# A two-layer decoder trunk on one core: memory gates computed in the order of use, value products on two PSUM tags, first query transpose one token block later

## The chip, the cores and the metric

The kernel runs on one core of a Trainium2 chip. The metric is the device time of one launch in microseconds, as the median of repeated runs. The core's engines are TensorE (PE in the profile; PEld is its weight load), VectorE (DVE), ScalarE (ACT), GpSimd (POOL) and SyncE (SP, which here only starts transfers).

## What is computed

One sequence of 1024 tokens with 1024 features goes through two layers. Both have memory cross-attention: 4 heads of width 128 in which every token reads 256 memory tokens, with a gate per token and feature behind it.

```python
def even_layer(h, mem, ...):          # layer 0
    u = rms_norm(h, norm_g)
    aq, ak, av, az, bh, bc, bb, bz, xq, xz = split(u @ w_in)
    ya = differential_attention(aq, ak, av, ...)    # 8 heads
    yb = short_gated_conv(bh, bc, bb, ...)
    yx = memory_cross_attention(xq, mem, ...)       # 4 heads
    y = concatenate([ya * silu(az), yb * silu(bz), yx * silu(xz)])
    return h + y @ w_out

def odd_layer(h, mem, ...):           # layer 1
    u = rms_norm(h, norm_g)
    cq, ck, cv, cz, cf, xq, xz = split(u @ w_in)
    yc = forgetting_attention(cq, ck, cv, cf, ...)  # 12 heads, q and k normalised
    yx = memory_cross_attention(xq, mem, ...)
    y = concatenate([yc * silu(cz), yx * silu(xz)])
    return h + y @ w_out

def memory_cross_attention(q, mem, mem_g, w_mem_kv, q_g, k_g):
    mk, mv = split(rms_norm(mem, mem_g) @ w_mem_kv)
    q, mk = rms_norm(q), rms_norm(mk)               # per head
    p = softmax(einsum('bshd,bmhd->bhsm', q, mk) * X_DIM ** -0.5)
    return einsum('bhsm,bmhd->bshd', p, mv)
```

## The kernel before

**Numbers and tiles.** Every fp32 operand of a product is split into a rounded high part and the rest (a cast by ACT, a subtraction by DVE or POOL, L130 and L131), and every product is three matmuls: high by high, high by low, low by high. L224 to L226 are the triple of a projection with tokens on the output's partitions (`token_unit`: 8 token blocks of 128, 8 triples each), L257 to L259 that of a projection with features on them (`feature_unit`: two halves of 512 tokens, 8 triples each, used for the gates), L417 the scores, L464 to L466 the value products, L786 to L788 the output projection.

**PSUM.** The 8 banks are dealt to four tags: d has three (projections and output projection), s two (scores), t two (transposes), o one (value products). Tiles of one tag take its banks in the order in which the program names them: a tile gets a bank when the tile that had it has been read, and no later tile of the tag overtakes it.

```python
PSUM_BUFS = {"d": 3, "s": 2, "t": 2, "o": 1}
o = self.bank("po", "o")                                   # pv, L441
```

**A memory pair** (`x_pair`, two pairs of two heads in each layer) projects the queries of both heads (8 token blocks, 128x256), computes both heads' gates (`gate_unit` to `gate_half`: a tanh `th` by ACT, L280, and a product into `xgate` by DVE, L281; the half with tokens 512 to 1023 first, that with tokens 0 to 511 second), and then attends in four groups g of 256 tokens, both heads in turn (`x_attend`). A group of a head is: two score triples, two row maxima (`nm`, DVE L654), two exponentials (`ex`, ACT L656), two reciprocals and scalings (DVE L658, L659), four transposes into one bank (`pt`, PE L451), its split (`pth` by ACT, `ptl` by DVE), six value matmuls into `po`, and `gated_y` (DVE L477), which multiplies `po` by `xgate` into `y`; a transfer from SP takes `y` to DRAM. The groups 0 and 1 need the gate's half of tokens 0 to 511.

**The order.** A scheduler with a timeline simulation of its own fixes each engine's order when the kernel is built: attention is preferred to projections (PRIO_ATT), evacuations of projections to both (PRIO_EVAC). On the chip each engine runs its list in that order and waits where an operand isn't there. While a pair's attention runs, the scheduler fills PE with the next projection: in pair 0 that of pair 1, in pair 1 the output projection.

**The end of layer 0.** While pair 1 runs, transfers bring the output weights in pieces (`wraw`), and ACT casts them into tiles that include the ones from which `u`, the layer's normalised input, was read for the last time (`u<-wraw`, L130). The output projection (`out_proj`) reads `y` back (`yr`), splits it (`yh`, `yl`), and its 24-matmul groups follow.

**The first head of layer 1.** `qkv_unit` projects q, k, v (and the forget logits: 396 columns for head 0) block by block. `evac` and `qk_norm` take a block out of PSUM and normalise it (ACT, DVE L294 and L297, POOL); behind each second block `later(DEFER, ...)` puts the transposes of both blocks (`qk_transpose`, PE L306, from `qr`) two groups of matmuls later. Here layer 0's last token block is still being turned (PE L148) while head 0 is projected: `turn_last`, behind the matmuls of block 2.

Of the kernel before, what the change touches and what calls it, by code (L numbers as in the profile page):

```python
# [7 lines left out]
F32 = mybir.dt.float32  # L8
# [7 lines left out]
P = 128  # L16
T = 1024
# [7 lines left out]
DEFER = 2  # L25
# [8 lines left out]
class Trunk:  # L34
# [178 lines left out]
    def token_unit(self, weights, lhs_hi, lhs_lo, nblk, post, together=False):  # L213

        nc = self.nc
        wh, wl = weights
        n = wh[0].shape[1]
        step = nblk if together else 1
        for t0 in range(0, nblk, step):
            blks = [(tb, self.bank("pd", "ds"[tb % 2] if together or self.boot else "d"), lhs_hi(tb), lhs_lo(tb)) for tb in range(t0, t0 + step)]  # L220
            for k in range(KC):
                h, l = wh[k], wl[k]
                for tb, ps, ah, al in blks:
                    nc.tensor.matmul(ps[:, :n], lhsT=ah(k), rhs=h, start=(k == 0), stop=False)  # L224
                    nc.tensor.matmul(ps[:, :n], lhsT=ah(k), rhs=l, start=False, stop=False)  # L225
                    mm = nc.tensor.matmul(ps[:, :n], lhsT=al(k), rhs=h, start=False, stop=(k == KC - 1))  # L226
            for tb, ps, _, _ in blks:
                with self.tc.high_priority(PRIO_EVAC):
                    post(tb, ps)
            if self.turn_last is not None and t0 == 2:  # L230
                with self.tc.issue_after(mm.ins):
                    self.turn_last()
                self.turn_last = None
            self.tick()

    def u_lhs(self, part):
        def f(tb):
# [23 lines left out]
                post(half, ps)  # L261
            self.tick()

    def gate_unit(self, w, c0, own=None):

        nc = self.nc
        if own is None:
            gate = {half: self.pk.tile([P, 512], F32, name="gate", tag="gate", bufs=2) for half in (1, 0)}
        else:
            gate = {half: own[:, half * 512:(half + 1) * 512] for half in (1, 0)}  # L270

        def post(half, ps):
            self.gate_half(gate[half], ps)
        self.feature_unit(w, c0, post, halves=(1, 0))
        return [gate[half][:, o:o + 256] for half in (0, 1) for o in (0, 256)]

    def gate_half(self, out, ps):
# [157 lines left out]
                                               op0=ALU.add, op1=ALU.max, accum_out=acc)  # L435
                prev[m] = acc

    def pv(self, g, es, vh, vl, nkb, causal):

        nc = self.nc  # L440
        o = self.bank("po", "o")  # L441
        for j in range(nkb // 2):
            pt = self.bank("pt", "t")
            last = causal and 2 * j + 2 == nkb
# [7 lines left out]
            w = 384 if last else 512  # L452
# [27 lines left out]
    def qkv_unit(self, w, cols, ng, gs, g, extra=None, pairs=False, weights=None):  # L480
        nc = self.nc
        qh, ql, kh, kl, vh, vl = self.att_tiles("qh", "ql", "kh", "kl", "vh", "vl")
# [3 lines left out]
        def post(tb, ps):  # L486
# [6 lines left out]
            if tb % 2:  # L493
                if pairs:
                    self.later(DEFER, lambda: self.qk_transpose_pairs(qns[tb - 1:tb + 1], (qh, ql), (kh, kd, kl, kz), g, (tb - 1) * P))
                else:
                    self.later(DEFER, lambda: self.qk_transpose(qns[tb - 1:tb + 1], [(qh, ql, g), (kh, kl, None)], (tb - 1) * P))
        if weights is None:
# [115 lines left out]
    def x_pair(self, layer, pr, w, cq, cz, w_out):  # L614
# [17 lines left out]
        for s, q in enumerate(((q0h, q0l), (q1h, q1l))):  # L632
            head = 2 * pr + s
            xh, xl = mem[s]
            vh, vl = [(lambda kb, v=v: v[:, M + kb * P:M + (kb + 1) * P]) for v in (xh, xl)]
            gate = self.gate_unit(w, cz + head * P, self.p1.tile([P, T], F32, name="xgate", tag="E2", bufs=2))
            heads.append((head, self.terms3(q, ([xh], [xl])), vh, vl, gate))
        if pr == 1:
            self.out_early(w_out)
# [6 lines left out]
    def x_attend(self, layer, g, head, terms, vh, vl, gate):  # L646
# [3 lines left out]
        for qb in (2 * g, 2 * g + 1):  # L650
# [7 lines left out]
            nc.vector.reciprocal(out=rl[:, 0:1], in_=ls[:, 0:1])  # L658
            nc.vector.tensor_scalar(out=e, in0=e, scalar1=rl[:, 0:1], scalar2=None, op0=ALU.mult)  # L659
            es.append(e)  # L660
        o = self.pv(g, es, vh, vl, 2, False)
        self.gated_y(layer, 12 + head, g, o, gate)


# [260 lines left out]
```

## Time and profile before

| | us |
|---|---|
| median of 3 runs (2204.52 to 2206.93) | 2206.74 |
| the profiled execution | 2204.26 |
| its span in the trace | 2202.2 |
| PE busy | 2167.8 (98%) |
| DVE, ACT, POOL busy | 1240.5, 1053.2, 1020.3 |

The mean granted clock of TensorE over the span is 0.996 of full speed. The page's chain of work that ended last runs through PE for 91% and through transfers for 4%. So PE sets the time, and what is left to look at are the stretches in which it waits: by stretches of 50 us, PE is busy for 50.00 of 50 nearly everywhere between 150 and 2150 us, and the exceptions are few. The kernel's places on that axis: the memory pairs of layer 0 from about 840 to 950, its output projection to about 1090, the first head of layer 1 from 1100, and the memory pairs of layer 1 from about 1945.

### The profile page before, as it was taken

The numbers are of one execution on the slowest core, as the hardware profiler recorded it, in microseconds if no ns is written. First come the engines' busy times: TensorE is split into PE (matmuls) and PEld (weight loads), VectorE is DVE, ScalarE is ACT, GpSimd is POOL, SyncE is SP. The second block draws the span as 40 slices with busy tenths as digits, with TensorE's granted clock in tenths as the row PEclk, the third lists the DMA queues.
The fourth block names the chain that finished last, engine by engine and source line by source line (L and its number), as shares of the span: only waits on it lengthen the run. The fifth ranks groups of instructions, "written<-read, shape, count | busy, mean of one in ns | idle before, by whom it ended". The sixth has DMA issues, their size and how long they took to land.

```text
span 2202.2 us, 35113 instructions
## 1 busy us (share of the span) xinstructions
PE 2167.8 (98%) x12528; PEld 1968.7 (89%) x12528; DVE 1240.5 (56%) x2864; ACT 1053.2 (48%) x2503; POOL 1020.3 (46%) x1352
## 2 busy tenths in 40 slices
PE   8999999999999999999999999999999999999999
PEld 7889889899898899778889999999999999998887
DVE  5656756665674677654445554554545555566532
ACT  6656455464554555433334444444444444455321
POOL 5565555555555454342334555544555554522100
PEclk9999999999999999999999999999999999999999
DMA  5450210211202112387521222201122220223743
GB/s 163 138 156 19 62 52 19 73 34 47 61 29 58 37 54 88 116 270 216 187 63 35 58 58 59 63 23 53 48 56 68 58 62 25 65 73 113 232 132 102
DMA packets 216983, 182.99 MB, mean 83 GB/s; under 512 B 19516, under 2 KB 174300, under 8 KB 216808
## 3 DMA queue, kind: packets, MB, share of 16 engines
q1 hardware_dynamic: 193768, 138.80, 21.6%
q10 hardware_dynamic: 23040, 41.95, 6.2%
q8 instruction: 98, 1.61, 0.3%
q14 instruction: 77, 0.63, 0.1%
HBM read 153.32 MB, written 27.38 MB: 82 GB/s over the span
## 4 chain that ended last, share of the span: by engine, by line
PE 91%; DMA 4%; DVE 1%; POOL 1%; ACT 1%; issue 1%; SPq 0%; ACTq 0%; POOLq 0%; DVEq 0%
PE pd L225 11%; PE pd L224 11%; PE pd L226 11%; PE pss L417 8%; PE pd L258 7%; PE pd L257 7%; PE pd L259 7%; PE pd L788 5%; PE pd L786 5%; PE pd L787 5%; PE pt L451 4%; PE po L466 2%; PE po L465 2%; PE po L464 2%; PE pt L306 1%; DMA wraw<-in_e_w_out_dram 1%
## 5 line engine op out<-in xcount | busy, mean ns | idle before, releaser
L224 PE MATMUL pd<-wqh,u 128*128 128x384 f32 (+2 forms) x1504 | 502.2, 335 | 0.7 <-ACT u L130 0.7
L225 PE MATMUL pd<-wql,u 128*128 128x384 f32 (+2 forms) x1504 | 500.8, 333 | 0.1
L226 PE MATMUL pd<-wqh,u 128*128 128x384 f32 (+2 forms) x1504 | 500.8, 333 | 0.0
L225 PEld LDWEIGHTS pd<-wql,u 128*128 128x128 f32 x1504 | 284.2, 189 | 5.8 <-DVE wql L131 0.6
L224 PEld LDWEIGHTS pd<-wqh,u 128*128 128x128 f32 x1504 | 284.1, 189 | 4.8 <-ACT u L130 1.1
L226 PEld LDWEIGHTS pd<-wqh,u 128*128 128x128 f32 x1504 | 283.7, 189 | 4.7 <-DVE u L131 0.2
L257 PE MATMUL pd<-u,wfh 128*128 128x512 f32 x704 | 279.0, 397 | 0.0
L258 PE MATMUL pd<-u,wfl 128*128 128x512 f32 x704 | 278.7, 396 | 0.0
L259 PE MATMUL pd<-u,wfh 128*128 128x512 f32 x704 | 277.8, 395 | 0.0
L131 POOL TENSOR_TENSOR wql<-raw,wqh 128x384 fp32r<-128x384 f32 (+2 forms) x214 | 210.2, 998 | 78.2 <-ACT wqh L130 73.5
L285 ACT ACTIVATE qr<-pd 128x384 f32<-128x384 f32 (+2 forms) x200 | 92.9, 468 | 199.4 <-PE pd L226 198.4
L131 DVE TENSOR_TENSOR yl<-yr,yh 128x512 fp32r<-128x512 f32 x128 | 103.7, 810 | 142.3 <-ACT yh L130 134.2
L124 POOL TENSOR_TENSOR rs_r<-rs_v,neghalf 128x2 f32<-128x2 f32 (+2 forms) x220 | 176.4, 802 | 12.8
L130 ACT ACTIVATE yh<-yr 128x512 fp32r<-128x512 f32 x128 | 80.5, 630 | 207.8 <-PE pd L787 113.4
L130 ACT ACTIVATE pth<-pt 128x512 fp32r<-128x512 f32 (+1 forms) x232 | 121.8, 554 | 112.5 <-PE pt L451 107.4
L131 POOL TENSOR_TENSOR vl<-qr,vh 128x128 fp32r<-128x128 f32 x160 | 79.0, 499 | 206.4 <-ACT vh L130 205.5
L723 POOL TENSOR_TENSOR fbias<-ck,cqn 128x896 f32<-128x896 f32 (+3 forms) x96 | 112.4, 1171 | 131.8 <-DVE mx L434 109.1
L297 DVE TENSOR_TENSOR qr<-qr,rs_r 128x256 f32<-128x256 f32 x200 | 123.5, 618 | 79.8 <-POOL rs_r L124 78.6
L131 POOL TENSOR_TENSOR wfl<-rawf,wfh 128x512 fp32r<-128x512 f32 x88 | 119.6, 1362 | 102.7 <-ACT wfh L130 100.2
L130 ACT ACTIVATE wqh<-raw 128x384 fp32r<-128x384 f32 (+2 forms) x252 | 114.7, 483 | 109.5 <-DMA raw<-in_e_w_in_dram 61.2
L131 DVE TENSOR_TENSOR ptl<-pt,pth 128x512 fp32r<-128x512 f32 (+1 forms) x232 | 143.8, 639 | 34.6 <-ACT pth L130 32.2
L259 PEld LDWEIGHTS pd<-u,wfh 128*128 128x128 f32 x704 | 132.7, 188 | 27.1 <-issue 1.1
(286 smaller groups left out, 5077.5 us busy)
## 6 DMA issues: line engine op xcount, KB each, us to landing
yr<-y_dr ACTq DMA_DIRECT2D x128, 256.0 KB
raw<-in_o_w_in_dram SPq DMA_DIRECT2D x96, 192.0 KB
rawf<-in_e_w_in_dram SPq DMA_DIRECT2D x56, 256.0 KB
y_dr<-y SPq DMA_DIRECT2D x112, 128.0 KB
raw<-in_e_w_in_dram SPq DMA_DIRECT2D x64, 192.0 KB
wraw<-in_e_w_out_dram SPq DMA_DIRECT2D x32, 256.0 KB
rn<-on_dr ACTq DMA_DIRECT2D x32, 256.0 KB
rawf<-in_o_w_in_dram SPq DMA_DIRECT2D x32, 256.0 KB
```

The source lines that it names most:

```text
L124: nc.gpsimd.tensor_tensor(out=r[:, :n], in0=v[:, :n], in1=self.neghalf[:, :n], op=ALU.pow)
L130: nc.scalar.activation(out=hi, in_=src, func=AF.Copy)
L131: lo_eng.tensor_tensor(out=lo, in0=src, in1=f32(hi), op=ALU.subtract)
L224: nc.tensor.matmul(ps[:, :n], lhsT=ah(k), rhs=h, start=(k == 0), stop=False)
L225: nc.tensor.matmul(ps[:, :n], lhsT=ah(k), rhs=l, start=False, stop=False)
L226: mm = nc.tensor.matmul(ps[:, :n], lhsT=al(k), rhs=h, start=False, stop=(k == KC - 1))
L257: nc.tensor.matmul(ps, lhsT=h, rhs=uh[:, k, :], start=(k == 0), stop=False)
L258: nc.tensor.matmul(ps, lhsT=l, rhs=uh[:, k, :], start=False, stop=False)
L259: nc.tensor.matmul(ps, lhsT=h, rhs=ul[:, k, :], start=False, stop=(k == KC - 1))
L297: nc.vector.tensor_tensor(out=v, in0=v, in1=r.unsqueeze(2).broadcast_to([P, ng, gs]), op=ALU.mult)
L417: nc.tensor.matmul(ps, lhsT=q[qb // 4][rows, qs], rhs=k[c0 // 512][rows, ks], start=(i == 0), stop=(i == n - 1))
L723: nc.gpsimd.tensor_tensor(out=b[:, :kext], in0=ck[:, :kext], in1=self.cqn[:, qb, h:h + 1].broadcast_to([P, kext]), op=ALU.subtract)
```

## The change

Three edits. (a) In `x_pair` the gates of the memory heads are computed with the half of tokens 0 to 511 first. (b) The value products of the odd head of each pair take a bank of tag d; those of the even head stay on o. (c) In the first head of layer 1, the transposes of token blocks 0 and 1 come one group later, and are issued behind that group's last matmul. What is computed stays the same, and so does the count of instructions on every engine.

```diff
--- before.py
+++ after.py
@@ -227,11 +227,17 @@
             for tb, ps, _, _ in blks:
                 with self.tc.high_priority(PRIO_EVAC):
                     post(tb, ps)
+            self.group_mm = mm
             if self.turn_last is not None and t0 == 2:
                 with self.tc.issue_after(mm.ins):
                     self.turn_last()
                 self.turn_last = None
             self.tick()
+
+    def behind_group(self, fn, *args):
+
+        with self.tc.issue_after(self.group_mm.ins):
+            fn(*args)
 
     def u_lhs(self, part):
         def f(tb):
@@ -261,7 +267,7 @@
                 post(half, ps)
             self.tick()
 
-    def gate_unit(self, w, c0, own=None):
+    def gate_unit(self, w, c0, own=None, halves=(1, 0)):
 
         nc = self.nc
         if own is None:
@@ -271,7 +277,7 @@
 
         def post(half, ps):
             self.gate_half(gate[half], ps)
-        self.feature_unit(w, c0, post, halves=(1, 0))
+        self.feature_unit(w, c0, post, halves=halves)
         return [gate[half][:, o:o + 256] for half in (0, 1) for o in (0, 256)]
 
     def gate_half(self, out, ps):
@@ -435,10 +441,10 @@
                                                op0=ALU.add, op1=ALU.max, accum_out=acc)
                 prev[m] = acc
 
-    def pv(self, g, es, vh, vl, nkb, causal):
-
-        nc = self.nc
-        o = self.bank("po", "o")
+    def pv(self, g, es, vh, vl, nkb, causal, tag="o"):
+
+        nc = self.nc
+        o = self.bank("po", tag)
         for j in range(nkb // 2):
             pt = self.bank("pt", "t")
             last = causal and 2 * j + 2 == nkb
@@ -493,6 +499,8 @@
             if tb % 2:
                 if pairs:
                     self.later(DEFER, lambda: self.qk_transpose_pairs(qns[tb - 1:tb + 1], (qh, ql), (kh, kd, kl, kz), g, (tb - 1) * P))
+                elif extra is not None and tb == 1:
+                    self.later(DEFER + 1, lambda: self.behind_group(self.qk_transpose, qns[tb - 1:tb + 1], [(qh, ql, g), (kh, kl, None)], (tb - 1) * P))
                 else:
                     self.later(DEFER, lambda: self.qk_transpose(qns[tb - 1:tb + 1], [(qh, ql, g), (kh, kl, None)], (tb - 1) * P))
         if weights is None:
@@ -633,7 +641,7 @@
             head = 2 * pr + s
             xh, xl = mem[s]
             vh, vl = [(lambda kb, v=v: v[:, M + kb * P:M + (kb + 1) * P]) for v in (xh, xl)]
-            gate = self.gate_unit(w, cz + head * P, self.p1.tile([P, T], F32, name="xgate", tag="E2", bufs=2))
+            gate = self.gate_unit(w, cz + head * P, self.p1.tile([P, T], F32, name="xgate", tag="E2", bufs=2), (0, 1))
             heads.append((head, self.terms3(q, ([xh], [xl])), vh, vl, gate))
         if pr == 1:
             self.out_early(w_out)
@@ -658,7 +666,7 @@
             nc.vector.reciprocal(out=rl[:, 0:1], in_=ls[:, 0:1])
             nc.vector.tensor_scalar(out=e, in0=e, scalar1=rl[:, 0:1], scalar2=None, op0=ALU.mult)
             es.append(e)
-        o = self.pv(g, es, vh, vl, 2, False)
+        o = self.pv(g, es, vh, vl, 2, False, "od"[head % 2])
         self.gated_y(layer, 12 + head, g, o, gate)
```

The edits move instructions in four places: the memory pairs of each layer with the start of the output projection, and the start of layer 1's head 0. The lines of the changed kernel stand 6 to 8 higher than those before (L230 to L232 for L224 to L226, L263 to L265 for L257 to L259, L312 for L306, L423 for L417, L457 for L451, L470 to L472 for L464 to L466, L794 to L796 for L786 to L788).

**PE, memory pair 0 of layer 0.** Before, where the attention of pair 0 begins to fill PE: `pss` are scores, `pt` transposes, and `pd<-wqh,u` the projection of pair 1's queries.

```order
L570 MATMUL psm<-sql,ones_r 2x256
L417 MATMUL pss<-vh,qh 128x256
L417 MATMUL pss<-vl,qh 128x256
L417 MATMUL pss<-vh,ql 128x256
L224 MATMUL pd<-wqh,u_130 128x256
L451 MATMUL pt<-ident,ex 128x128 x4
L417 MATMUL pss<-vh,kh 128x256
L417 MATMUL pss<-vl,kh 128x256
L417 MATMUL pss<-vh,kl 128x256
L225 MATMUL pd<-wql,u_130 128x256
L226 MATMUL pd<-wqh,u_132 128x256
```

Now, at the same place; `po` are the value products, of both heads.

```order
L423 MATMUL pss<-vh,ql 128x256
L457 MATMUL pt<-ident,ex 128x128 x4
L423 MATMUL pss<-vh,kh 128x256
L423 MATMUL pss<-vl,kh 128x256
L423 MATMUL pss<-vh,kl 128x256
L470 MATMUL po<-pth,vh 128x256
L471 MATMUL po<-pth,vl 128x256
L470 MATMUL po<-pth,vh 128x256
L471 MATMUL po<-pth,vl 128x256
L472 MATMUL po<-ptl,vh 128x256
L470 MATMUL po<-pth,vh 128x256
L471 MATMUL po<-pth,vl 128x256
```

What moved: the matmuls of pair 1's projection, which stood between the attention's groups from here on, 1 to 19 at a time, now all stand behind the last value products of pair 0, 91 instructions later, since their tiles of tag d come behind the four `po` of the odd head. In layer 1's pair 0 it is the same, with 72 instructions.

**ACT, the last gate of layer 0.** Before: `u00` and `u01` are casts of output weights that wait for a transfer, `th_11293` is the last gate half.

```order
L130 ACTIVATE u00_11659<-wraw_11808 128x512
L130 ACTIVATE u00_11659<-wraw_11812 128x512
L130 ACTIVATE u00_11659<-wraw_11816 128x512
L280 ACTIVATE th_11293<-pd_11268 128x512
L778 DMA rn_11706<-on_dr0_111 128x512
L778 DMA rn_11727<-on_dr0_111 128x512
L778 DMA rn_11764<-on_dr1_112 128x512
L130 ACTIVATE u01_11660<-wraw_11856 128x512
L130 ACTIVATE u01_11660<-wraw_11860 128x512
L130 ACTIVATE pth_11515<-pt_11510 128x512
```

Now:

```order
L130 ACTIVATE u00_11659<-wraw_11808 128x512
L130 ACTIVATE u00_11659<-wraw_11812 128x512
L130 ACTIVATE u00_11659<-wraw_11816 128x512
L286 ACTIVATE th_11293<-pd_11268 128x512
L786 DMA rn_11706<-on_dr0_111 128x512
L130 ACTIVATE pth_11557<-pt_11552 128x512
L786 DMA rn_11727<-on_dr0_111 128x512
L130 ACTIVATE u01_11660<-wraw_11856 128x512
L130 ACTIVATE pth_11599<-pt_11594 128x512
```

What moved: `th_11293`, now the half of tokens 512 to 1023, still stands behind the same casts; the copies `pth` of the last attention groups follow it earlier. On PE the output projection now starts behind all value products; before, four groups of six were left at its start.

**PE, the first head of layer 1.** Before, at the turn of the last token block (`xn`) and the first transpose of queries (`qr`):

```order
L226 MATMUL pd<-wqh,u_12471 128x396
L148 MATMUL pt<-ident,xn_13331 128x128 x8
L306 MATMUL pt<-ident,qr 128x128
L224 MATMUL pd<-wf_12872,u_12469 128x396
L225 MATMUL pd<-wf_12873,u_12469 128x396
```

Now:

```order
L226 MATMUL pd<-wqh,u_12471 128x396
L148 MATMUL pt<-ident,xn_13331 128x128 x8
L224 MATMUL pd<-wf_12872,u_12469 128x396
L225 MATMUL pd<-wf_12873,u_12469 128x396
L226 MATMUL pd<-wf_12872,u_12471 128x396
```

and 24 matmuls later:

```order
L225 MATMUL pd<-wql,u_12469 128x396
L226 MATMUL pd<-wqh,u_12471 128x396
L312 MATMUL pt<-ident,qr 128x128
L224 MATMUL pd<-wf_12872,u_12470 128x396
L225 MATMUL pd<-wf_12873,u_12470 128x396
```

What moved: the 24 matmuls of token block 3 now stand between the turn and the first transpose of `qr`.

## Rows read from the trace of the kernel before

**Rows 1.** The page, part 1: busy us (share of the span) of each engine.

```profile
PE 2167.8 (98%) x12528; PEld 1968.7 (89%) x12528; DVE 1240.5 (56%) x2864; ACT 1053.2 (48%) x2503; POOL 1020.3 (46%) x1352
```

**Rows 2.** 50-us stretches: PE, PEld, DVE, ACT, POOL busy; clock, DMA share, GB/s.

```profile
900.00:950.00 50.00, 44.72 (x211) 37.12 (x211) 27.20 (x47) 19.66 (x42) 19.98 (x14) 0.90 0.53 171
950.00:1000.00 50.00, 46.62 (x198) 36.42 (x197) 29.14 (x30) 20.31 (x35) 24.22 (x17) 1.00 0.93 301
1100.00:1150.00 50.00, 45.90 (x235) 41.75 (x234) 20.43 (x33) 17.77 (x39) 18.12 (x25) 0.97 0.24 69
```

**Rows 3.** Timeline of PE where layer 0 ends (start, us, instruction, [idle before]).

```profile
916.99 0.60 PE L451 MATMUL pt<-ident,ex 128*128 128x128 f32 x4
921.25 0.58 PE L464 MATMUL po<-pth,kd 128*128 128x256 f32 x1 [3.66 <-DVE y L477]
926.61 0.78 PE L786 MATMUL pd<-kd,yh 128*128 128x512 f32 x1
```

**Rows 4.** Timeline of ACT at the same place.

```profile
917.62 1.27 ACT L130 ACTIVATE u<-wraw 128x512 fp32r<-128x512 f32 x2 [0.79 <-DMA wraw<-in_e_w_out_dram]
918.79 0.58 ACT L280 ACTIVATE th<-pd 128x512 f32<-128x512 f32 x1
```

**Rows 5.** Three stretches of 2 us, columns as in rows 2.

```profile
918.00:920.00 2.00, 0.00 (x0) 0.00 (x0) 1.19 (x2) 1.36 (x3) 1.27 (x1) 0.93 0.61 176
928.00:930.00 2.00, 1.91 (x5) 1.53 (x6) 2.00 (x5) 0.63 (x1) 2.00 (x2) 0.51 0.82 282
96.00:98.00 2.00, 0.31 (x3) 0.10 (x1) 0.77 (x1) 0.62 (x4) 0.80 (x2) 1.00 0.91 291
```

**Rows 6.** Timelines of PE and, last, DVE at layer 1's first query transpose.

```profile
1138.84 0.45 PE L306 MATMUL pt<-ident,qr 128*128 128x128 f32 x1 [4.10 <-DVE qr L297]
1139.74 0.53 PE L226 MATMUL pd<-wf,u 128*128 128x396 f32 x1
1141.66 0.35 PE L226 MATMUL pd<-wf,u 128*128 128x396 f32 x1
...
1137.89 0.81 DVE L297 TENSOR_TENSOR qr<-qr,rs_r 128x256 f32<-128x256 f32 x1
```

**Rows 7.** Timeline of DVE in the first memory pair of layer 0.

```profile
858.52 1.74 DVE L131 TENSOR_TENSOR we<-wraw,we 128x512 fp32r<-128x512 f32 x1 [0.46 <-ACT we L130]
860.52 0.67 DVE L131 TENSOR_TENSOR ptl<-pt,pth 128x512 fp32r<-128x512 f32 x1
861.12 0.41 DVE L654 TENSOR_REDUCE nm<-pss 128x1 f32<-128x256 f32 x1
861.45 0.15 DVE L658 RECIPROCAL rl<-ls 128x1 f32<-128x1 f32 x1
861.63 0.36 DVE L659 TENSOR_SCALAR ex<-ex,rl 128x256 f32<-128x256 f32 x1
861.95 0.42 DVE L294 TENSOR_REDUCE qk_ms<-sq 128x2 f32<-128x256 f32 x1
862.29 0.41 DVE L477 SCALAR_TENSOR_TENSOR y<-po,xgate 128x256 f32<-128x256 f32 x1
```

**Rows 8.** Timeline of PE in the same stretch.

```profile
856.52 0.28 PE L465 MATMUL po<-pth,vl 128*128 128x256 f32 x1
856.64 0.28 PE L466 MATMUL po<-ptl,vh 128*128 128x256 f32 x1
862.04 0.60 PE L451 MATMUL pt<-ident,ex 128*128 128x128 f32 x4
862.40 0.36 PE L417 MATMUL pss<-vh,qh 128*128 128x256 f32 x1
```

**Rows 9.** 10 us in the first memory pair of each layer, columns as above.

```profile
850.00:860.00 10.00, 10.00 (x86) 9.89 (x85) 7.58 (x17) 8.16 (x22) 7.39 (x8) 1.00 0.69 204
1952.00:1962.00 10.00, 10.00 (x87) 10.00 (x86) 8.06 (x25) 6.09 (x18) 3.52 (x4) 1.00 0.36 118
```

**Rows 10.** Timeline of PE in layer 0's output projection.

```profile
970.75 0.50 PE L786 MATMUL pd<-u,yh 128*128 128x512 f32 x1 [1.62 <-ACT yh L130]
```

## The prediction

> **What bounds the kernel now.** I read the page first: PE is busy for 2167.8 of 2202.2 us [rows 1], so a change that leaves every matmul in place can only win back PE's idle time, 34 us in all, and the time that it ran at the lower clock, or lose by making new idle time. The stretches of 50 us show where that idle time lies. Three of them bear on this change [rows 2]: 900 to 950 (PE idle 5.28 us, clock 0.90), 950 to 1000 (idle 3.38 us, clock 1.00, DMA share 0.93) and 1100 to 1150 (idle 4.10 us, clock 0.97). The timeline of PE then names the waits in them. At the end of layer 0, PE waits 3.66 us for a `y` [rows 3], and the output projection starts at 926.61; the rest of the 5.28 us are smaller gaps around it. At the first query transpose of layer 1 it waits 4.10 us for `qr` [rows 6]. The clock fell after both: it was 0.93 in the two microseconds in which PE did nothing, and 0.51, the 1.2 GHz level, in 928 to 930, in which PE was busy for 1.91 of 2 [rows 5]. The places that matter most for the sum, though, are those where nothing is idle yet: in the first memory pair of either layer PE is busy for 10.00 of 10 us, while DVE is busy for 7.58 and 8.06 [rows 9].
>
> **Part (c), the first query transpose.** It is taken out from behind the turn of the last block, and 24 matmuls of 396 columns come ahead of it. One of 256 columns goes by in 0.12 us (856.52 to 856.64) [rows 8], so one of 396 in about 0.18, and the 24 in 4.4 us. PE is free at 1138.84 - 4.10 = 1134.74 and reaches the transpose at 1139.1 instead; `qr` is there at 1137.89 + 0.81 = 1138.70 [rows 6]. So the whole 4.10 us goes. The slow clock behind it goes too: from 1139.74 to 1141.66 there are 6 matmul pitches of 0.32 us instead of 0.18 [rows 6], nine matmuls in all ran so, hence 9 x 0.14 = 1.3 us. What is late next is block 3's own `qr`, which the next transposes need; they stand a further group on, so I put 0.4 us for it. Sum -5.0 us; between -5.6 and -3.5 if a wait of up to 2 us stays.
>
> **Parts (a) and (b), the end of layer 0.** Before, both heads share one bank for `po`, and the groups 0 and 1 wait for the gate's half that comes last. That half's `th` starts on ACT at 918.79, 1.8 us after PE was done with its matmuls (916.99), because ACT was in casts of output weights that themselves waited for transfers [rows 3, 4]. Now the half needed first is computed first, and the last half is needed by two groups of one head only. But that half's `th` still stands behind the same casts, as the pieces of ACT's order show, and so do, with casts that wait between them, the last three `pth`. Counted from the end of the gate's first half, I follow ACT's rows to the same start of the output projection, about 16.5 us later, as before. PE's work in front of that start grows by 28 instructions (24 value matmuls and 4 transposes, 24 x 0.12 + 0.36 = 3.2 us [rows 8]), but 16 of these (6 scores, 6 value matmuls, 4 transposes, 1.8 us) lie ahead of the point from which I count. So only 3.2 - 1.8 = 1.4 us of idle time is filled. The bounds are 0 (nothing but a shift) and 8.8 us: all 5.28 us of idle, and the lower clock from 921.25 to about 930, where 7.1 us of work would take 3.5 us less.
>
> **The output projection of layer 0.** Before, the last `y` were written while the projection ran, and the SP queue held weight loads behind them. Now all `y` are out before it, so later weights can be asked for sooner. The waits in 950 to 1000 are 3.38 us [rows 2], the longest 1.62 for `yh` [rows 10]. Against it, ACT's list now has the casts of the second half's weights further forward, ahead of some `yh`, in a stretch whose DMA share is 0.93 [rows 2]. I take -1.5 us; bounds -3.4 (all of it) and +4 (two more waits for a cast of the size of the one in [rows 10], and a little).
>
> **Part (b), the first memory pair of layer 0.** Here the change costs. Tiles of tag d take turns, and the four `po` of the odd head now stand in front of pair 1's projection. That projection filled PE between the attention's steps; now 91 instructions of attention stand alone. Their matmul time is 67 x 0.12 for scores and value products, plus six sets of transposes at 0.36: 10.2 us [rows 8]. What feeds them is DVE. From the place that was 850.13 before, to the last value products, DVE has in its order 6 `ptl`, 7 `nm`, 9 reciprocals, 9 scalings, 6 `y`, two weight casts and one `xgate`. Their pitches in the timeline are 0.60, 0.33, 0.18, 0.32 and 0.33; the casts take 0.7 to 1.7 each, and `xgate` as long as a `ptl` [rows 7]. That makes 3.6 + 2.3 + 1.6 + 2.9 + 2.0 + 2.4 + 0.6 = 15.4 us; where a scaling follows another, its pitch is shorter, so I take 15.0. With the last split and eight value matmuls behind it, 16.3 us pass until the projection starts, against 10.2 us of PE work: 6.1 us of new idle time, in gaps of up to 1.6 us. Bounds: 4.5 us (the casts at their shorter time, a few matmuls hidden better) and 8 us (each group also waits for ACT's exponential). Nothing gives it back later, because behind this place PE was never idle up to 916.99.
>
> **The first memory pair of layer 1.** The same with 72 instructions: 8.0 us of matmuls against 12.0 us of DVE and ACT steps, summed in the same way: 4.0 us, bounds 3.0 and 5.5. The end of layer 1 had no waits for `y` to win back, so there I put 0 (-0.5 to +0.5).
>
> **Would the clock fall there?** The gaps in the two new stretches are up to 1.6 us. In 96 to 98 PE was busy for 0.31 of 2 us, and the granted clock stayed 1.00 [rows 5]; so I keep the full clock, and add nothing. The Trainium skill speaks against this, on its page "TensorE: Matmul & The Clock Gate", section "A second HAM failure mode: psum-queue depth-cycling": a kernel that cycles through PSUM banks lets TensorE idle briefly between groups often enough that its clock swings between the two levels. By that rule the two stretches would run at 1.2 GHz and the time be about 2217 (an estimate from the rows, rival 2) instead of 2209; the row of 96 to 98 shows one gap without a fall, not a series of them, so it doesn't refute the rule, and it is a rival below.
>
> **Sum.** -5.0 - 1.4 - 1.5 + 6.1 + 4.0 = +2.2 us on the profiled execution: 2204.26 becomes 2206.5. That execution was 2.48 us under the median of the three runs, so against the median 2206.74 I get about 2209, 0.1% more. A measurement of this kernel can tell about 0.2%, 4.4 us, from no change; the forecast is within it.
>
> **Rivals.**
> 1. The pairs fill better and layer 0's end gains more. It needs the last `pth` not to wait for the casts, so that 5 us instead of 1.4 is won, and the pairs at their lower bounds: -5.0 - 5.0 - 1.5 + 4.5 + 3.0 = -4.0, or 2202.7; with -8.8 for the end, 2199. For it speaks that the `y` that PE waited for is no longer needed there; against it that ACT's casts wait for transfers, which no edit changes. Chance 0.2; three quarters of it lie beyond -0.2%.
> 2. Slower, by the clock. In the pairs, a series of gaps lowers the clock to 1.2 GHz. Work of 10.2 and 8.0 us would take 20.4 and 16.0, more than the 16.3 and 12.0 us of the steps that feed it: +4.1 and +4.0, which makes 2217. It decides if the clock falls within the first third of a stretch; if it falls late, half of that, 2213. Against it stands the row of 96 to 98. Chance 0.2.
> 3. Slower, by the weights. The casts that now stand ahead of `yh` wait for transfers at a DMA share of 0.93, at the +4 end: +5.5 over my sum, 2214.5. Chance 0.1.
> 4. The change doesn't do what it says at layer 0's end: `th` stays behind the casts, and the wait is only renamed. Without the 1.4, 2210.4; within 0.2%. Chance 0.1.
>
> **How the numbers follow.** The forecast itself (2202.3 to 2211.2) has 0.4. Faster by over 0.2%: 0.15, from rival 1. Slower: rivals 2 and 3 with 0.3. Within 0.2%: 0.4, rival 4 and the rest of rival 1, 0.55. The range leaves out about one in ten on either side: 2200 to 2217.
>
> **What would show it.** In the profile of the changed kernel: no wait at the first query transpose over 0.5 us, and 1100 to 1150 with PE busy for over 49.5 and the clock at 1.00; in the first pair of layer 0 PE idle for 4.5 to 8 us where it was full, with waits of value products and transposes for DVE and ACT, and for 3 to 5.5 us in that of layer 1; at layer 0's end a wait for `ptl` or `pth` in the place of that for `y`, and the clock low there once more. I am wrong if the pairs stay full (then d's banks were no limit), if their clock is under 1.00, or if the wait at layer 0's end is gone altogether.

## The result: 0.2% slower, the forecast time with other terms

The changed kernel takes 2208.54 us (median of 21 runs, 2206.11 to 2211.93) beside 2205.04 us for the kernel before (21 runs, 2200.18 to 2208.92): a ratio of 1.0017, 95% interval 1.001 to 1.0023. In a second measurement beside other kernels the ratio was 1.0028, 1.0018 to 1.0038. So it is slower by 0.1 to 0.4%. The forecast was about 2209 us and "within 0.2%", with 0.3 for slower by more: the first ratio lies just within that, the second just beyond it. The profiled execution took 2209.09 us, its span is 2207.3 (before: 2204.26 and 2202.2).

First three stretches of 50 us in the kernel before that [rows 2] doesn't have (columns as there), all full, then the stretches of the changed kernel.

```profile
850.00:900.00 50.00, 50.00 (x398) 48.58 (x397) 37.93 (x103) 29.29 (x84) 16.74 (x24) 1.00 0.24 73
1950.00:2000.00 50.00, 50.00 (x385) 47.95 (x384) 36.15 (x100) 27.64 (x78) 11.62 (x20) 1.00 0.15 47
2000.00:2050.00 50.00, 50.00 (x250) 42.21 (x249) 26.77 (x45) 21.26 (x41) 9.53 (x7) 1.00 0.50 153
```

```profile
850.00:900.00 50.00, 44.77 (x348) 42.81 (x348) 33.16 (x92) 26.38 (x75) 15.57 (x22) 0.97 0.24 71
900.00:950.00 50.00, 46.03 (x231) 38.85 (x230) 30.81 (x57) 22.27 (x48) 18.85 (x15) 0.93 0.50 159
950.00:1000.00 50.00, 49.55 (x215) 39.44 (x214) 27.46 (x31) 19.86 (x34) 23.37 (x17) 1.00 0.95 312
1100.00:1150.00 50.00, 49.90 (x261) 45.06 (x260) 23.14 (x40) 21.06 (x47) 20.97 (x30) 1.00 0.28 79
1950.00:2000.00 50.00, 48.15 (x353) 45.06 (x354) 31.82 (x90) 25.02 (x70) 10.46 (x19) 0.97 0.14 43
2000.00:2050.00 50.00, 47.93 (x247) 40.70 (x246) 31.35 (x57) 27.51 (x54) 15.96 (x12) 1.00 0.66 211
```

PE now idles 5.23 us in 850 to 900, 1.85 in 1950 to 2000 and 2.07 in 2000 to 2050. It has won back 1.31 us in 900 to 950, 2.93 in 950 to 1000 and 4.00 in 1100 to 1150. The waits that came in (line waited for: us in total, times, longest) are of the value products and their transposes, for ACT and DVE:

```profile
PE po L470 <- ACT pth L130: 7.6, 5, 2.2
PE po L472 <- DVE ptl L131: 2.8, 4, 1.3
PE pt L457 <- DVE rl L666: 1.6, 1, 1.6
```

To see the terms apart, I cut both traces of PE at instructions with the same work ahead of them (but for a few transposes): the first matmul into `psm` (181.8 us before), the last 128x256 projection matmul of layer 0 (890.5), the first `xn` transpose in its output projection (1047.0), the end of block 3 in layer 1's head 0 (1144.6), the last 128x256 projection matmul of layer 1 (1987.5) and the last output matmul (2198.1). The stretch ahead of the first cut is left out: its idle time differs from run to run.

| us from cut to cut | before | changed | difference | forecast |
|---|---|---|---|---|
| to the last projection of layer 0 (its pair 0) | 708.7 | 717.0 | +8.3 | +6.1 |
| to the middle of its output projection (its end) | 156.5 | 151.6 | -4.9 | -2.9 |
| to the first queries' transpose of layer 1 | 97.6 | 91.9 | -5.7 | -5.0 |
| to the last projection of layer 1 (its pair 0) | 842.9 | 849.3 | +6.4 | +4.0 |
| to the end (end of layer 1) | 210.5 | 211.7 | +1.2 | 0 |
| sum | | | +5.3 | +2.2 |

**The first pair of layer 0.** The timeline of PE (start, us, instruction, idle before it) and, below, stretches of 2 us there and in layer 1's first pair, with the granted clock before the DMA share:

```profile
851.35 0.28 PE L423 MATMUL pss<-vh,kl 128*128 128x256 f32 x1
852.87 0.39 PE L470 MATMUL po<-pth,vh 128*128 128x256 f32 x1 [1.24 <-ACT pth L130]
857.82 0.39 PE L472 MATMUL po<-ptl,vh 128*128 128x256 f32 x1 [1.27 <-DVE ptl L131]
866.04 0.95 PE L457 MATMUL pt<-ident,ex 128*128 128x128 f32 x4 [1.62 <-DVE rl L666]
867.23 0.41 PE L472 MATMUL po<-ptl,vh 128*128 128x256 f32 x1
867.44 0.41 PE L470 MATMUL po<-pth,vh 128*128 128x256 f32 x1
```

```profile
864.00:866.00 2.00, 0.42 (x3) 0.18 (x3) 0.76 (x4) 0.69 (x3) 0.00 (x0) 1.00 0.25 74
866.00:868.00 2.00, 1.89 (x10) 1.73 (x11) 1.23 (x3) 0.60 (x1) 0.00 (x0) 0.70 0.21 66
868.00:870.00 2.00, 2.00 (x12) 2.00 (x10) 0.74 (x2) 0.00 (x0) 0.00 (x0) 0.50 0.16 49
870.00:872.00 2.00, 2.00 (x18) 2.00 (x18) 0.00 (x0) 0.00 (x0) 0.00 (x0) 0.95 0.08 21
1952.00:1954.00 2.00, 2.00 (x11) 2.00 (x11) 1.49 (x6) 1.54 (x6) 0.57 (x1) 0.56 0.92 263
1954.00:1956.00 2.00, 2.00 (x12) 1.72 (x10) 2.00 (x7) 0.71 (x3) 0.72 (x1) 0.59 0.50 191
```

The attention stands alone and PE waits for its steps, as forecast. (The last four value matmuls stand behind the first 22 matmuls of pair 1's projection, so not all value products come ahead of it, as the section on the change has it.) The last gap is 1.62 us, and after it the clock fell: 0.50 in 868 to 870, the 1.2 GHz level, with PE busy for 2.00 of 2. Value matmuls then follow each other at 0.21 us (867.23 to 867.44) instead of 0.12 [rows 8]. In layer 1's pair the clock fell to about half at 1952 to 1956, behind one gap of 1.79 us.

**The end of layer 0.** PE and ACT, which answer to [rows 3, 4]:

```profile
930.88 0.39 PE L470 MATMUL po<-pth,kd 128*128 128x256 f32 x1 [2.19 <-ACT pth L130]
932.54 0.58 PE L472 MATMUL po<-ptl,kd 128*128 128x256 f32 x1 [1.15 <-DVE ptl L131]
937.32 0.79 PE L794 MATMUL pd<-kd,yh 128*128 128x512 f32 x1
```

```profile
928.43 0.63 ACT L130 ACTIVATE u<-wraw 128x512 fp32r<-128x512 f32 x1 [1.51 <-DMA wraw<-in_e_w_out_dram]
929.76 0.58 ACT L286 ACTIVATE th<-pd 128x512 f32<-128x512 f32 x1
```

The last gate half's tanh (929.76) still stands behind casts that wait for `wraw`; the wait for `y` has become waits for `pth` and `ptl`. The output projection starts at 937.32, 16.9 us after the end of the gate's first half (920.4); the forecast had 16.5, as before. What got better lies mostly behind it. Here is the queue of SP before, and then after (start, us, transfer that is issued):

```profile
933.57 18.65 SPq L473 DMA_DIRECT2D y_dr<-y  x4
952.31 2.52 SPq L808 DMA_DIRECT2D hb<-in_x_dram  x4
```

```profile
942.92 0.39 SPq L479 DMA_DIRECT2D y_dr<-y  x1
943.39 5.91 SPq L816 DMA_DIRECT2D hb<-in_x_dram  x4
```

Before, the last four stores of `y` held the queue for 18.65 us, to 952, and the loads behind them (`hb`, `wraw`) started 26 us after the output projection. Now they start 6 us after it.

**The first query transpose.** It comes 24 matmuls later and without a wait, where [rows 6] had 4.10 us; the row for `xn` is the one ahead of the 24:

```profile
1136.75 1.04 PE L148 MATMUL pt<-ident,xn 128*128 128x128 f32 x8
1141.99 0.27 PE L312 MATMUL pt<-ident,qr 128*128 128x128 f32 x1
```

### The profile page after: what moved, and what is told of

It is laid out like the page before. It is cut to its first block, busy times and chain, and to the rows that moved or that the text cites. A ratio compares the mean times of both kernels' runs of the same rounds, so it can differ in the third digit from the quotient of the medians.

```text
span 2207.3 us, 35144 instructions
## 1 busy us (share of the span) xinstructions
PE 2171.7 (98%) x12528; PEld 1970.1 (89%) x12528; DVE 1236.2 (56%) x2864; ACT 1056.1 (48%) x2503; POOL 1021.2 (46%) x1352
## 4 chain that ended last, share of the span: by engine, by line
PE 91%; DMA 4%; DVE 1%; ACT 1%; POOL 1%; issue 1%; SPq 0%; ACTq 0%; POOLq 0%; DVEq 0%
PE pd L224 12%; PE pd L225 12%; PE pd L226 12%; PE pss L423 7%; PE pd L264 7%; PE pd L265 7%; PE pd L263 7%; PE pd L794 5%; PE pd L796 5%; PE pd L795 5%; PE pt L457 4%; PE po L472 2%; PE po L471 2%; PE po L470 2%; PE pt L312 1%
## 5 line engine op out<-in xcount | busy, mean ns | idle before, releaser
L224 PE MATMUL pd<-wqh,u 128*128 128x384 f32 (+2 forms) x1504 | 501.7, 334 | 1.4 <-ACT u L130 0.8
L226 PE MATMUL pd<-wqh,u 128*128 128x384 f32 (+2 forms) x1504 | 500.3, 333 | 0.0
L224 PEld LDWEIGHTS pd<-wqh,u 128*128 128x128 f32 x1504 | 284.2, 189 | 5.8 <-ACT u L130 1.6
L226 PEld LDWEIGHTS pd<-wqh,u 128*128 128x128 f32 x1504 | 283.7, 189 | 4.6 <-DVE u L131 0.2
L263 PE MATMUL pd<-u,wfh 128*128 128x512 f32 x704 | 278.7, 397 | 0.0
L265 PE MATMUL pd<-u,wfh 128*128 128x512 f32 x704 | 277.2, 394 | 0.0
L265 PEld LDWEIGHTS pd<-u,wfh 128*128 128x128 f32 x704 | 132.3, 188 | 27.2 <-issue 1.1
```

What stands on the lines that cost most here:

```text
L263: nc.tensor.matmul(ps, lhsT=h, rhs=uh[:, k, :], start=(k == 0), stop=False)
L265: nc.tensor.matmul(ps, lhsT=h, rhs=ul[:, k, :], start=False, stop=(k == KC - 1))
```

## Experiments

All ratios are to the kernel before on the same chip, with 95% intervals. Stage times are cut as in the table above.

**(c) alone.** The kernel before with only this edit (and the helper `behind_group`; dots mark what is left out):

```diff
+                elif extra is not None and tb == 1:
+                    self.later(DEFER + 1, lambda: self.behind_group(self.qk_transpose, ...))
```

> Part (c) alone: the kernel before, with the transposes of the first query blocks of layer 1 one group later; nothing else moves. My theory: the wait of 4.1 us and the slow clock behind it go, and PE, which is busy without a gap behind that place, keeps the whole gain: 5 to 5.6 us faster than before (ratio 0.9974 to 0.9978), stretch 1100 to 1150 busy for over 49.5, stretches 850 to 1000 as in the kernel before. Rival: the gain is given back in later waits, 0 to 2 us faster (0.999 to 1.000).

Measured: 2197.17 us, 0.9964 (0.9952 to 0.9977), so 5 to 10.6 us faster. In the trace the stage takes 91.9 us instead of 97.6, and the stages behind it 1053.4 as before (1053.5). Nothing is given back. The stretches of layer 0's end are as before:

```profile
900.00:950.00 50.00, 44.99 (x212) 37.76 (x211) 25.03 (x42) 19.17 (x38) 19.97 (x14) 0.90 0.57 173
950.00:1000.00 50.00, 45.65 (x190) 34.52 (x190) 28.63 (x30) 19.72 (x35) 24.70 (x17) 1.00 0.93 299
1100.00:1150.00 50.00, 49.90 (x264) 45.58 (x263) 21.63 (x38) 19.69 (x45) 19.23 (x27) 1.00 0.25 69
```

**(a) and (c), without (b).** All value products on tag o:

```diff
-        o = self.pv(g, es, vh, vl, 2, False, "od"[head % 2])
+        o = self.pv(g, es, vh, vl, 2, False)
```

> Parts (a) and (c) without (b): all value products on tag o again. My theory, that the turns of tag d cost the time in the first memory pairs: PE is busy for 50.0 in 850 to 900 again and without a gap in the first pair of layer 1; the end of layer 0 gains 0 to 3 us from the order of the gates, as the last gate half stands behind only two more casts that wait for transfers; with (c) 5 to 8.5 us faster than before (ratio 0.996 to 0.9978). Rival, that the order of the gates packs the attention of the first pair and so opens the gaps: PE idle for 4 to 6 us in 850 to 900 here too, and the time within 2 us of the kernel before.

Measured: 2192.32 us, 0.9938 (0.9924 to 0.9951), 13.4 us faster than the kernel before and the fastest kernel here. Run once more as a measure for other kernels:

> The kernel with (a) and (c) without (b) once more, as the measure for the two beside it. It was at 2192.3 us, ratio 0.9938 to before; the same is expected, between 0.992 and 0.9955.

it gave 2192.09 us, 0.9937 (0.9925 to 0.995).

```profile
850.00:900.00 50.00, 50.00 (x396) 48.40 (x395) 38.26 (x105) 29.13 (x83) 16.24 (x23) 1.00 0.24 73
950.00:1000.00 50.00, 48.89 (x214) 39.64 (x213) 27.90 (x30) 18.08 (x32) 24.57 (x17) 1.00 0.91 294
1950.00:2000.00 50.00, 50.00 (x360) 46.84 (x360) 32.83 (x96) 25.87 (x74) 10.04 (x18) 1.00 0.09 28
```

The first pairs are full in both layers, so the order of the gates doesn't pack the attention: the rival falls. And the end of layer 0 gains by (a) alone: the second stage takes 151.7 and 149.1 us in the two runs, against 156.5 before and 158.4 with (c) alone. That is more than the 0 to 3 us that I had put for it; two executions of this one kernel differ there by 2.6 us. The last store of `y` leaves SP's queue at 938.5 and `hb` follows at 938.95, 13.5 us after the projection's start at 925.4.

**(b) in the second pairs alone, with (a) and (c).**

```diff
+        o = self.pv(g, es, vh, vl, 2, False, "od"[head % 2] if head > 1 else "o")
```

> The change with part (b) for the second memory pair of each layer alone; in the first pair all value products are on tag o. My theory: the first pairs stay full (PE 50.0 in 850 to 900), the gain of about 5 us that the changed kernel shows from the end of layer 0 through 950 to 1000 stays, and so does the new wait of some 2 us at the end of layer 1: -5.6 -4.9 +2 = 8 to 9 us faster than before (ratio 0.996, between 0.9950 and 0.9970). Rival: what is won at the end of layer 0 is only the gaps of the first pair given back (its transfers had had more time), then -5.6 and 0 to +2: ratio 0.9975 to 0.9985.

Measured: 2196.84 us, 0.9962 (0.995 to 0.9975). The first pairs are full again (708.5 and 843.6 us). The time lies in the range that I had put, but not for the reason: it is 4.5 us slower than (a) and (c) without (b). The end of layer 1 takes 213.4 us instead of 209.5, that of layer 0 153.1 instead of 149.1 to 151.7, which is little more than two executions differ by. So the second bank wins nothing at either end and costs at the second; what I had put down to (a) and (b) together is (a).

**(b) and (c), without (a).**

```diff
-            gate = self.gate_unit(w, cz + head * P, ..., (0, 1))
+            gate = self.gate_unit(w, cz + head * P, ...)
```

> Parts (b) and (c) without (a): the gates' half of tokens 512 to 1023 first again. My theory: the first pairs lose as in the changed kernel (PE idle for about 5 us in 850 to 900, clock under 1.00 there), since that is (b). At the end of layer 0 the half that is computed last is again the one that the first groups need, so the wait for y is back and 2 to 4 us of the gain there go: 2 to 4 us slower than the changed kernel, ratio to before 1.0025 to 1.0035. Rival, that (a) has no part in it and the gain at the end of layer 0 is all from the second bank: as the changed kernel, 1.0012 to 1.0022.

Measured: 2219.1 us, 1.0061 (1.0049 to 1.0074): 10 us slower than the changed kernel, more than expected. The first pair loses in the same way (715.8 us), the end of layer 0 takes 159.4 us, 8 more than in the changed kernel, and that of layer 1 215.6 us. The low clock that I had expected in the first pair didn't come. PE's last wait in it:

```profile
864.54 0.92 PE L457 MATMUL pt<-ident,ex 128*128 128x128 f32 x4 [1.22 <-DVE rl L666]
```

and the stretch of 2 us behind it:

```profile
866.00:868.00 2.00, 2.00 (x18) 1.84 (x17) 1.02 (x2) 0.15 (x1) 0.00 (x0) 1.00 0.01 4
```

The order of PE is that of the changed kernel, the waits are the same to 0.1 us but for the last (1.22 instead of 1.62), and here the clock stayed at 1.00. From these last transposes to the ninth matmul of the projection behind them the same work took 2.96 us here (864.54 to 867.50) and 4.17 in the changed kernel (866.04 to 870.21), so the fall of the clock cost about 1.2 us. The length of the gap doesn't explain it: in a second execution of the changed kernel the gap at this place was 1.13 us, shorter than here, and the clock fell all the same.

```profile
866.03 0.92 PE L457 MATMUL pt<-ident,ex 128*128 128x128 f32 x4 [1.13 <-DVE rl L666]
```

```profile
868.00:870.00 2.00, 2.00 (x12) 2.00 (x11) 0.69 (x2) 0.00 (x0) 0.00 (x0) 0.50 0.19 56
```

**A second bank that belongs to tag o**, with (a) and (c):

```diff
-PSUM_BUFS = {"d": 3, "s": 2, "t": 2, "o": 1}
+PSUM_BUFS = {"d": 2, "s": 2, "t": 2, "o": 2}
```

> (a) and (c), and a second bank for all value products that belongs to tag o itself, taken from d (d 2, s 2, t 2, o 2). My theory, that (b) costs because value products take turns with projections in one tag: here they don't, so the first memory pairs keep PE busy (idle under 1 us in 850 to 900 and in the first pair of layer 1, clock 1.00), and the end of layer 0 is as with (a) and (c) or better: ratio to before 0.991 to 0.996. Rival 1: a second bank as such packs the attention and drains the fill: idle of 3 us or more in the first pairs. Rival 2: two banks are too few for the projections: PE idles between token blocks all through the kernel, ratio over 1.00.

Measured: 2276.19 us, 1.0316 (1.0302 to 1.033). The first pairs are nearly as my theory has it, and two banks for the projections are too few, as the second rival has it. The stretch with the first pair of layer 0:

```profile
850.00:900.00 50.00, 48.86 (x341) 44.72 (x340) 30.89 (x83) 27.85 (x73) 18.02 (x21) 1.00 0.30 91
```

and the waits of PE in the whole kernel:

```profile
PE pt L312 <- DVE qr L303: 20.6, 13, 2.1
PE pd L263 <- DVE gate L287: 9.6, 9, 1.6
```

In 850 to 900 PE idles 1.14 us; none of its waits there is for `pth` or `ptl`. A second bank alone doesn't drain the fill. This fits that the turns of tag d do, though the test isn't a clean one: d has lost a bank here, and the scheduler's order is another one in this stretch. But with two banks on d, PE waits 13 times for `qr` and 9 times for a gate, 30 us in all.

**The tanh ahead of the casts.** I had put the wait at layer 0's end down to ACT's casts. Here the casts of the weights' pieces 8 and up are ordered behind the last gate's tanh, once with (a) and (c), once in the changed kernel:

```diff
+            if half == 0 and c >= CUT:                       # CUT = 8; the rest as before
+                with self.tc.issue_after(self.gate_th.ins):
+                    nc.scalar.activation(out=tiles(0, c), in_=raw, func=AF.Copy)
```

> (a) and (c) without (b), and in addition ACT's casts of the output weights' pieces 8 and up are ordered behind the tanh of the last gate half (they may read no earlier; nothing else is forced). My theory, that this tanh and with it the last y are held by casts that wait for transfers: the two waits for y at the end of layer 0 (1.75 and 1.07 us in the kernel without this order) go, and a part of the low clock behind them: 2 to 5 us faster than (a) and (c) alone, ratio to before 0.9915 to 0.993. Rival: the output projection then waits for the pieces cast later, as all stand behind the same transfers: within 1.5 us of (a) and (c) alone, or slower.

> The changed kernel, all three parts, with the same order of ACT's casts behind the last gate's tanh. My theory: the waits for pth and ptl at the end of layer 0 (2.19 and 1.15 us) and at the end of layer 1 (2.07 us) are those casts, so both go, with a part of the slow clock at 932 to 938: 3 to 7 us faster than the changed kernel, ratio to before 0.998 to 1.000; the first pairs lose as they do there. Rival: the transfers themselves set the end of the layer, and the waits move to yh or to the weights: within 1.5 us of the changed kernel.

Measured: 2194.89 us, 0.9945 (0.9933 to 0.9958), not faster than (a) and (c) at 0.9937; and 2214.85 us, 1.0041 (1.0027 to 1.0055), not faster than the changed kernel. My theory falls: the casts do hold the tanh, but they are not what the time hangs on. The first time is where the rival of that run has it (within 1.5 us or slower); whether it is late weights that cost, as the rival says, no run shows. PE, then DVE, at layer 0's end in the first of the two:

```profile
923.42 0.55 PE L471 MATMUL po<-pth,kd 128*128 128x256 f32 x1 [2.86 <-DVE y L484]
```

```profile
922.85 0.43 DVE L484 SCALAR_TENSOR_TENSOR y<-po,xgate 128x256 f32<-128x256 f32 x1 [3.10 <-DMA y_dr<-y]
```

and at layer 1's end in the second:

```profile
2024.54 0.55 PE L471 MATMUL po<-pth,vh 128*128 128x256 f32 x1 [3.41 <-DVE y L484]
```

```profile
2022.44 0.42 DVE L484 SCALAR_TENSOR_TENSOR y<-po,xgate 128x256 f32<-128x256 f32 x1 [1.83 <-DMA y_dr<-y]
```

The tanh is early now, and DVE waits for a transfer instead: `y` has two buffers, and the store of the older one is still under way.

**Four buffers for y** in the second pairs (those of `qr`, free by then): with (a) and (c), with the tanh first as well, and in the changed kernel with the tanh first.

```diff
+        if chunk > 13:
+            y = self.p1.tile([P, self.wq_n], F32, name="qr", tag="qr", bufs=4)[:, :256]
+        else: ...                                                     # as before
```

> (a) and (c) without (b), and the y of the second memory pairs rotate through four buffers (the free ones of qr) instead of two. New theory: behind the tanh there is a second limit of the same length, the two buffers of y, which DVE may write again only when the transfer of an older y to DRAM is done (DVE waited 1.5 and 2.7 us for it in the two runs of (a) and (c)). Expected: that wait goes, 0.5 to 2.5 us faster than (a) and (c), ratio to before 0.9925 to 0.994. Rival: the output projection waits for what comes back from DRAM anyway: same as (a) and (c), 0.9937.

> As the last one, with the casts of the output weights also ordered behind the last gate's tanh. New theory: with the tanh first alone, PE waited 2.86 us for a y whose buffer was still being sent (DVE waited 3.1 us for that transfer); with four buffers the order of the casts pays: 2 to 5 us faster than with the tanh first alone (0.9945), ratio to before 0.992 to 0.9935, and not slower than four buffers alone. Rival: the casts behind the tanh make the weights late and that is what cost: ratio 0.994 to 0.995 again.

> The changed kernel with the tanh first and four buffers for the y of the second pairs. New theory: with the tanh first alone it was slower (1.0041) because DVE then waited for y buffers (2.7 us at the end of layer 0, and up to 2.7 at the end of layer 1, where PE waited 3.41 us for y and its clock fell); with four buffers these waits go: 5 to 9 us faster than that, ratio to before 1.000 to 1.002, at or under the changed kernel. Rival: the second bank lets value products run ahead of the casts in any case: within 2 us of 1.0041.

> The changed kernel once more, as the measure for the one beside it: ratio to before 1.001 to 1.0025.

Measured: 2191.49 us, 0.9943 (0.9929 to 0.9957); 2192.28 us, 0.9943 (0.9929 to 0.9956); 2212.36 us, 1.0033 (1.0021 to 1.0046); the changed kernel again 2209.44 us, 1.0028 (1.0018 to 1.0038). Buffers alone can't be told from (a) and (c). With the tanh first they took 2.6 us off the end of layer 0 in the trace (154.4 to 151.8) and 4.3 off that of layer 1 in the changed kernel (219.0 to 214.7), but the ratios, 0.9945 to 0.9943 and 1.0041 to 1.0033, don't separate that from nothing, and neither kernel is faster than the one without both edits. The new theory isn't borne out. With tanh and buffers out of the way PE waits at the start of the output projection:

```profile
923.42 0.50 PE L803 MATMUL pd<-kd,yh 128*128 128x512 f32 x1 [2.73 <-ACT yh L131]
```

So at the end of layer 0 the traces show three limits of nearly the same length one behind the other: the tanh (with (a) and (c), PE waits 1.75 and 1.07 us for a `y`), the buffers of `y` (2.86 us), and `yh`, the first operand of the projection (2.73 us). Taking two away won nothing that could be measured. What `yh` waits for in the end (its transfer or POOL's product ahead of it) I haven't tried.

## Why the forecast held, and where its steps were off

The time is as forecast, but in part by luck. By the medians the change costs 3.5 us where I had 2.2, and the base that I started from, 2206.7, is 1.7 us above the median of 21 runs, so two errors cancel. Between the two traces the sum is +5.3; the profiled execution of before lies 0.8 us under its median, that of the changed kernel 0.6 above. Inside the sum errors cancel too: the first pairs cost 14.7 us where I had 10.1, and layer 0's end and part (c) won 10.6 where I had 7.9. The side of the boundary is close: 0.17% in one measurement, 0.28% in the other. And one of the signs that I had named for being wrong came, a clock under 1.00 in the first pairs (0.97 in 850 to 900 and in 1950 to 2000).

- **Part (c)**: -5.7 against -5.0. The whole wait and the slow clock went; the 0.4 us that I put for the next wait weren't needed (0.10 us idle in 1100 to 1150).
- **Part (b), first pair of layer 0**: +8.3 against +6.1, just over my upper bound of 8. That (b) is the cause is shown by the full pairs without it, and the second bank in a tag of its own fits the turns of tag d. Three things were mis-sized. The stretch took 18.7 us until the projection, where I had 16.3, since I summed DVE's steps without the waits between them. The longest is one that I had left out: DVE stands for 1.39 us at a `y` whose buffer is still being stored, and the `rl` that PE waits 1.62 us for comes behind it in DVE's order.

```profile
865.21 0.42 DVE L483 SCALAR_TENSOR_TENSOR y<-po,xgate 128x256 f32<-128x256 f32 x1 [1.39 <-DMA y_dr<-y]
```

  Of the 8.5 us over PE's 10.2 us of work the brackets hold only 4.96: PE's rows last 0.28 us and follow each other every 0.12, so each gap is about 0.16 us longer than its bracket (851.35 to 852.87 is 1.52; less one pitch of 0.12 that is 1.40, and the bracket says 1.24). And the clock fell, for which I had added nothing on the strength of one gap without a fall [rows 5]. That was weak ground: in the changed kernel's profile PE waits 1.51 us at the same place (to 98.00; before, 1.76), and there the clock did fall behind it:

```profile
100.00:102.00 2.00, 2.00 (x11) 2.00 (x11) 1.74 (x6) 1.78 (x7) 1.84 (x4) 0.50 0.54 166
```

- **First pair of layer 1**: +6.4 against +4.0, over the bound of 5.5, and by another wait than I had. The 72 instructions took 14.3 us until the projection (1947.69 to 1961.97), where I had 12.0. But PE's bracketed waits there are 2.0 us in all, under the 3 to 5.5 that I had named as a sign: 0.23 and 1.79, and the long one is for a `pth` that stands behind a cast of output weights in ACT's order, which waits for its transfer (PE, then ACT):

```profile
1951.50 0.39 PE L470 MATMUL po<-pth,vh 128*128 128x256 f32 x1 [1.79 <-ACT pth L130]
```

```profile
1950.33 0.63 ACT L130 ACTIVATE we<-wraw 128x512 fp32r<-128x512 f32 x1 [1.26 <-DMA wraw<-in_o_w_out_dram]
```

  Behind it the clock fell, which cost at most 1.7 us (0.44 and 0.41 of 2 us in the rows of 1952 to 1956). The rest stands in no bracket.
- **End of layer 0**: the start of the output projection came as worked out, and with it the small gain ahead of it (2.7 us later, with 3.2 us of work moved in front of it: -0.5 against -1.4). The gain behind it is -4.4, against -1.5 with a bound of -3.4. The step that failed is the choice between the ends: of the waits for `yh` that I feared, none is left in 950 to 1000, whose idle time is 0.45 us. Of the 4.4 us, 2.65 are idle time (3.66 us from the projection's start to the cut before, 1.01 now) and about 1.1 the low clock, which now ends sooner behind that start (0.67 over the first 5 us before, 0.89 now). SP's queue was free 20 us sooner relative to the projection, but that this is the cause isn't shown: no run changes the queue alone, and with `hb` 13.5, 13.4 and 12.5 us behind the start, PE idled 1.45 and 0.00 us there in two executions of (a) and (c), and 3.26 without (a). I also gave the gain to (a) and (b) together; it is (a), and (b) wins nothing there.
- **End of layer 1**: I put 0, since before had no wait there. With two banks the value products run ahead to where ACT's casts hold the tanh, as in layer 0:

```profile
2024.66 0.39 PE L470 MATMUL po<-pth,vh 128*128 128x256 f32 x1 [2.07 <-ACT pth L130]
```

```profile
2021.29 0.63 ACT L130 ACTIVATE u<-wraw 128x512 fp32r<-128x512 f32 x1 [1.11 <-DMA wraw<-in_o_w_out_dram]
2022.54 0.58 ACT L286 ACTIVATE th<-pd 128x512 f32<-128x512 f32 x1
```

The rows are of PE and ACT. With (b) in the second pair alone this end lost 3.9 us against (a) and (c).

Of the rivals, the fall of the clock was real but cost less than the +4 us for each pair that I had put: about 1.2 us in the first, at most 1.7 in the second, since it was short and, in the first, came behind the last gap. The Trainium skill, page "TensorE: Matmul & The Clock Gate", section "A second HAM failure mode: psum-queue depth-cycling", says that brief idling between groups that cycle through PSUM banks can make the clock swing between its levels. The traces agree in part: the clock fell in each first pair of the changed kernel, but once each and not in swings, at 866 to 872 and, behind a single long gap, at 1952 to 1956; and it didn't fall in the first pair of layer 0 in the kernel without (a), with nearly the same gaps.

## What to carry to other kernels

Before a second kind of tile is given banks of a rotating tag, ask what else takes turns there: a slow user in front of the filler work takes that work away from the engine, even where banks are free in time. Undo each edit of a change alone before judging it: two of these three edits win 13 us together, and the third costs more than that. And where a wait is removed, look at the next limit behind it before building on the gain; at the end of layer 0 there were three of nearly one length.

## What was not expected of the hardware

- The stretch ahead of 150 us differs between executions of one program: PE idled 17.2 us in it in the profile of before, and 17.7 and 19.7 in two profiles of the changed kernel. The last two differ by as much as a change of 0.1%, so such a change is better read between cuts behind it.
- The clock's fall isn't the same in each execution or order: in the first pair of layer 0, with the same matmuls in the same order, it went to 0.50 behind last gaps of 1.62 and 1.13 us (two executions of the changed kernel) and stayed at 1.00 behind one of 1.22 (the kernel without (a)). Behind the gap that ends at 98 us it fell in the profile of the changed kernel (1.51 us) and not in that of before (1.76).
- SP's queue stood for 18.65 us over four stores of `y`, 15.6 of them in waits for DVE. With that, PE idled 3.38 and 4.35 us in 950 to 1000 (before, and (c) alone); where the stores went out earlier, 0.45 us (the changed kernel), 1.11 and 0.00 (two executions of (a) and (c)), but also 2.24 with (b) in the second pairs alone, so this isn't the only thing that it hangs on.
